# The decoder layer: the parts of x stored once and loaded by later stages, queries and keys transposed before they are split

## The chip, the cores and the metric

One Trainium2 chip, of which the kernel uses one core. The metric is the time of one execution on the device in microseconds (us); lower is better. Three runs of the kernel before took 1255.81, 1256.64 and 1258.46 us, median 1256.64.

Engine names are those of the profile: PE is TensorE's matmul, PEld its weight load, DVE VectorE, ACT ScalarE, POOL GpSimd, SP SyncE, from which all transfers (DMAs) of this kernel are issued.

## The reference

One decoder layer over 2048 tokens, model width 1024, head width 64. Both mixers have eight heads; mixer A has two heads of keys and values.

```python
hdn  = rmsnorm(x, norm_gain)
proj = einsum("bsd,de->bse", hdn, w_in)
q_a, k_a, v_a, g_a, q_b, k_b, v_b, g_b = split(proj)
q, k = rope(rmsnorm(q, ...)), rope(rmsnorm(k, ...))      # per head, both mixers
o_a = banded_attention(q_a, k_a, v_a, 127, sinks) * silu(g_a)
o_b = dilated_attention(q_b, k_b, v_b) * silu(g_b)       # (128,1), (512,4), (2048,16), merged
out = x + einsum("bse,ed->bsd", concat([o_a, o_b]), w_out)
```

Mixer A is causal attention with a window of 128 tokens and a learnt sink per head. Mixer B attends under three pairs of window and stride; the three results are merged by weights from their softmax denominators.

## The kernel before, in words

**Two parts for each operand.** A matmul takes each float32 operand as a high part, rounded to fp32r, and a low part, the rest. One product is three matmuls, high by high, high by low and low by high (`mm3`, L241 to L244). Everything that goes into a matmul is thus split first: the high part by a copy on ScalarE, the low part by a subtraction.

**Stages.** The work runs in eight stages: four of mixer B (a pair of heads each), two of mixer A (four query heads each) and two of the output projection (half of the output's columns each). A stage goes through four blocks `sb` of two halves; a half `hf` is 256 tokens, so a stage has eight halves. In a half, for each 128 tokens (`tt`), the projection takes eight chunks of x with three matmuls of 384 columns each (L244), and then the gates are made in the same way with 256 columns, once in B and twice in A.

**x.** x comes transposed from `in_xT`. `x_load` (L145 to L149) loads four chunks of a half into the tile `xs` (512 KB, two loads a half; in the output stages from the mixers' results `mx`), and `x_split` (L151 to L158) makes `xh` on ScalarE and `xl` on GpSimd or, for the second half of the chunks, in halves 0 to 5, on VectorE: four splits of 128x512 a half. Each stage loads and splits x anew for itself, one half ahead of its use. `xs` has two buffers, `xh` and `xl` six each. The very first half is split in `first_half`.

**Queries and keys.** `norm_rope` (L406) squares the projected values and applies the rotary tables (result `t1`, called t in the profile); `norm_factors` (L434) makes the factors `fac` of the per-head norm by a power on GpSimd (L182); `norm_split` (L441) multiplies `t1` by them on VectorE (L447) and splits the result into the tile `hl`, high parts on ScalarE (L456 queries, L457 keys, twice each), low parts on GpSimd (L458, L459). `qk_transposes` (L463) then transposes the parts on TensorE by the fp32r identity `idr`: in B four blocks for each 128 tokens (L475) and two for the low keys (L499); in A four (L485) and two (L490, L491) for each 128 tokens. ScalarE moves the transposed parts from PSUM (tile `po`) into `Q`, `qc`, `KK` and `klz` (L477, L478, L487, L493, L494, L502). In A, `klz` (`KL` in the code) has keys in one half of the partitions only. GpSimd also casts `Q` into `qc` in B (L479).

**Order.** The transposes of a half run in `finish`, which is deferred into the next half, behind its projection. Attention runs as a pipeline of units that `advance` slips between the projection's steps; the cost of a stage (`pcost`) sets how fast. A scheduler puts each engine's instructions into a fixed order when the kernel is built; all transfers stand in one queue of SP. Scores are L590 and L591 (windows) and L808 and L809 (strides), the probabilities' transposes L619, L625, L719, L828 (fp32, by `idf`), their parts L573 and L574 (`pth`, `ptl`).

**Others.** Weights come in `stg` tiles (three buffers) and are split into `wh`, `wl`. The three results of mixer B are merged on GpSimd with rows of weights that are written to DRAM (`rD`) and read back into all partitions (`Rb`): `o1c` by `Rb` (L899), `osum` by `Rb` (L904), their sum (L905), and the product with the gate (L906). At the start, GpSimd also clears the `klz` tiles (L90).

Of the kernel before, what the change touches and what calls it, by code (L numbers as in the profile page):

```python
# [21 lines left out]
XB = 6  # L22
# [6 lines left out]
def f32(ap):  # L29
    return ap.bitcast(F32)  # L30
# [3 lines left out]
def hybrid_layer(ctx, tc, xT, xn, x, wB, wA, wO, ng, gains, sinks, rot, masks, ident, out):  # L34
# [16 lines left out]
    idr = const.tile([128, 128], F32R, name="idr")  # L51
# [21 lines left out]
    def late_constants(part):  # L73
# [5 lines left out]
        nc.scalar.activation(idr, idf, AF.Copy)  # L79
# [12 lines left out]
    rs_row = [dram([256], f"rsr{hf}") for hf in range(8)]  # L92
    mx = [dram([128, KC, 256], f"mx{hf}") for hf in range(8)]
# [50 lines left out]

    def x_load(si, hf, g):  # L145
        src = mx[hf] if STAGES[si][0] == "O" else xT[hf]
        f = xp.tile([128, 4, 256], F32, name="xs")
        nc.sync.dma_start(f, src[:, 4 * g:4 * g + 4, :])
        XS[si, hf, g] = f  # L149

    def x_split(si, hf, g):  # L151
        f = XS[si, hf, g // 2][:, 2 * (g % 2):2 * (g % 2) + 2]
        h = xp.tile([128, 2, 256], F32R, name="xh", bufs=XB)
        l = xp.tile([128, 2, 256], F32R, name="xl", bufs=XB)
        nc.scalar.activation(h, f, AF.Copy)  # L155
        eng = nc.gpsimd if g < 2 or hf >= 6 else nc.vector
        eng.tensor_tensor(l, f, f32(h), op=OP.subtract)  # L157
        XG[si, hf, g] = (h, l)  # L158

    def first_half():  # L160
        for g in range(4):
            if g % 2 == 0:
                XS[0, 0, g // 2] = xp.tile([128, 4, 256], F32, name="xs")
            f = XS[0, 0, g // 2][:, 2 * (g % 2):2 * (g % 2) + 2]
            h = xp.tile([128, 2, 256], F32R, name="xh", bufs=XB)
            l = xp.tile([128, 2, 256], F32R, name="xl", bufs=XB)
# [4 lines left out]
            XG[0, 0, g] = (h, l)  # L171
# [74 lines left out]
    def proj(si, sb):  # L246
# [22 lines left out]
        for half in range(2):  # L269
            hf = 2 * sb + half  # L270
            nx = next_half(si, hf)
            xg = [XG.pop((si, hf, g)) for g in range(4)]
            TC, TS = TB.pop((si, hf))
            if nx:
                x_load(*nx, 0)
            t1s = []
            un = wk.tile([128, 2, nh], F32, name="un")
            for tt in range(2):
# [12 lines left out]
                if tt == 0 and nx:  # L291
                    x_load(*nx, 1)
# [44 lines left out]
            hls = norm_split(kind, nq, nk, t1s, fac)  # L337
            if si == 0 and hf < 7:
                rb_make(hf + 1)
            deferred.append(lambda half=half, hls=hls: finish(si, sb, half, hls))  # L340

    def finish(si, sb, half, hls):
# [3 lines left out]
        if half == 0 and sb > 0:  # L346
# [3 lines left out]
            for h in range(nk):  # L350
                hs = slice(64 * h, 64 * h + 64)
                nc.scalar.activation(KL[hs, h, :, 0, :], f32(pl[hs, h, :, 4, :]), AF.Copy)
        yield from qk_transposes(si, sb, half, hls)
# [87 lines left out]
    def norm_split(kind, nq, nk, t1s, fac):  # L441
        nh = nq + nk
        n = nh * 64
        hls = []
        for tt, t1 in enumerate(t1s):
            t1v = t1[:, :n].rearrange("p (h d) -> p h d", d=64)
            nc.vector.tensor_tensor(t1v, t1v, fac[:, tt, :, None].to_broadcast([128, nh, 64]), op=OP.mult)  # L447
            hl = wk.tile([128, 11, 64], F32R, name="hl", bufs=2)
            k0 = 2 * nq
            if kind == "A":  # L450
                hi, lo = hl[:, 0:8:2, :], hl[:, 1:8:2, :]
            else:
                hi, lo = hl[:, 0:4:3, :], hl[:, 1:3, :]
            khi = hl[:, k0:k0 + 2 * nk, :].rearrange("p (h a) d -> p h a d", a=2)
            klo = hl[:, k0 + 2 * nk:k0 + 3 * nk, :]
            nc.scalar.activation(hi, t1v[:, :nq], AF.Copy)  # L456
            nc.scalar.activation(khi, t1v[:, nq:, None, :].to_broadcast([128, nk, 2, 64]), AF.Copy)  # L457
            nc.gpsimd.tensor_tensor(lo, t1v[:, :nq], f32(hi), op=OP.subtract)  # L458
            nc.gpsimd.tensor_tensor(klo, t1v[:, nq:], f32(khi[:, :, 0, :]), op=OP.subtract)  # L459
            hls.append(hl)  # L460
        return hls

    def qk_transposes(si, sb, half, hls):  # L463
        kind, _ = STAGES[si]
        KK, KL = K[si, sb]
        q = Q[si, sb]
        i0 = 2 * half

        for tt, hl in enumerate(hls):
            i = i0 + tt  # L470
            if kind == "B":
                blocks = [hl[:, 2 * b:2 * b + 2, :] for b in range(4)]
# [567 lines left out]
```

## Time and profile before

| | |
|---|---|
| median of three runs | 1256.64 us |
| the profiled execution's own time | 1261.51 us |
| its span in the profile | 1259.4 us |
| mean granted TensorE clock | 0.969 |
| busy: PE, DVE, ACT, POOL | 1174.8, 850.7, 834.7, 680.4 us |
| loaded and stored by the SP queue | 219.37 MB |

How to read it: the span is one execution, taken by the hardware profiler; busy times are sums over an engine's instructions, of which many lie beside one another. The stages begin at about 0, 151, 314, 487, 661, 866, 1045 and 1156 us (first projection of the stage). A wait's row names the waiting engine, its instruction and what ended the wait, then the sum in us, the number and the longest. A group's row has the line, the engine, the operation, output and inputs with partitions x elements and type, the count, then the sum in us and the mean in ns of one, then the idle time ahead of them. Matmuls' ends are modelled, so that starts are the better reading. The granted clock is a share of full speed.

### The profile page before, as it was taken

What the parts mean: (1) busy time and instruction counts of PE and PEld (TensorE: products, weight loads), DVE (VectorE), ACT (ScalarE), POOL (GpSimd) and SP (SyncE); (2) the same over time, 40 slices, a digit from 0 to 9 for tenths busy, and PEclk for the clock granted to TensorE, in tenths of its full rate; (3) what the DMA queues carried; (4) which work ended last, traced back from release to release, by engine and by line L of the source; (5) the groups of instructions that cost most, each with busy time, mean ns of one, the idle gap of its engine ahead of it and who ended that gap; (6) DMA issues with size and microseconds to landing.
All of it is one profiled execution on the core that took longest, in us unless ns stands there. A gap on an engine that the chain in (4) does not pass through costs nothing.

```text
span 1259.4 us, 25438 instructions
## 1 busy us (share of the span) xinstructions
PE 1174.8 (93%) x8328; PEld 1141.3 (91%) x8328; DVE 850.7 (68%) x2288; ACT 834.7 (66%) x2418; POOL 680.4 (54%) x788
## 2 busy tenths in 40 slices
PE   6898979899899798899998999999999999999899
PEld 5898979899799798888997999898899998999898
DVE  5676768678677678776777788789868877522221
ACT  6477868678677687676777677677776776522221
POOL 4886734566645574536576567565655554333122
PEclk9899989999899899899998999999999999999999
DMA  7454677877687667687775764545333225566561
GB/s 215 120 166 127 193 226 212 229 200 212 182 250 207 210 190 201 189 244 204 199 210 172 228 203 143 150 137 167 114 97 94 80 89 165 163 192 211 166 191 69
DMA packets 196883, 220.98 MB, mean 175 GB/s; under 512 B 34312, under 2 KB 143632, under 8 KB 196752
## 3 DMA queue, kind: packets, MB, share of 16 engines
q1 hardware_dynamic: 196752, 219.37, 59.3%
q8 instruction: 66, 1.08, 0.4%
q14 instruction: 65, 0.53, 0.1%
HBM read 164.44 MB, written 54.86 MB: 174 GB/s over the span
## 4 chain that ended last, share of the span: by engine, by line
PE 55%; DMA 16%; DVE 10%; ACT 8%; POOL 6%; issue 3%; SPq 2%; POOLq 0%; ACTq 0%; DVEq 0%
PE pj L244 39%; DMA xs<-in_xT 3%; DMA Rb<-rD 2%; DMA stg<-in_wB 2%; PE po L849 2%; DMA stg<-in_wO 2%; DMA stg<-in_wA 2%; PE sc L590 1%; PE sc L591 1%; PE po L645 1%; PE pt L828 1%; PE po L735 1%; PE pt L719 1%; ACT P L599 1%; DVE ptl L574 1%
## 5 line engine op out<-in xcount | busy, mean ns | idle before, releaser
L244 PE MATMUL pj<-wh,xh 128*128 128x384 f32 (+1 forms) x1008 | 332.8, 332 | 12.2 <-ACT wh L104 5.5
L244 PE MATMUL pj<-wl,xh 128*128 128x384 f32 (+1 forms) x1008 | 334.4, 332 | 0.8 <-DVE wl L102 0.7
L244 PE MATMUL pj<-wh,xl 128*128 128x384 f32 (+1 forms) x1008 | 333.4, 331 | 1.3 <-DVE xl L157 1.3
L157 POOL TENSOR_TENSOR xl<-xs,xh 128x512 fp32r<-128x512 f32 x158 | 210.3, 1341 | 146.3 <-ACT xh L155 136.6
L155 ACT ACTIVATE xh<-xs 128x512 fp32r<-128x512 f32 x252 | 154.5, 629 | 123.6 <-PE pj L244 100.6
L244 PEld LDWEIGHTS pj<-wh,xh 128*128 128x128 f32 x1008 | 194.0, 193 | 15.7 <-ACT wh L104 5.8
L244 PEld LDWEIGHTS pj<-wl,xh 128*128 128x128 f32 x1008 | 194.8, 193 | 3.2 <-DVE wl L102 1.1
L244 PEld LDWEIGHTS pj<-wh,xl 128*128 128x128 f32 x1008 | 194.4, 193 | 3.0 <-DVE xl L157 1.6
L574 DVE TENSOR_TENSOR ptl<-pt,pth 128x512 fp32r<-128x512 f32 (+3 forms) x232 | 142.0, 619 | 35.5 <-ACT pth L573 31.8
L244 PE MATMUL pj<-xh,wgh 128*128 128x256 f32 x496 | 147.7, 298 | 17.9 <-DVE V L311 12.0
L244 PE MATMUL pj<-xh,wgl 128*128 128x256 f32 x496 | 145.8, 294 | 0.0
L244 PE MATMUL pj<-xl,wgh 128*128 128x256 f32 x496 | 145.4, 293 | 0.0
L573 ACT ACTIVATE pth<-pt 128x512 fp32r<-128x512 f32 (+3 forms) x232 | 123.1, 543 | 23.1 <-PE pt L719 8.1
L431 POOL TENSOR_TENSOR t<-t,t 128x256 f32<-128x256 f32 (+1 forms) x96 | 78.1, 814 | 77.9 <-DVE t L422 57.2
L244 PEld LDWEIGHTS pj<-xh,wgh 128*128 128x128 f32 x496 | 97.8, 197 | 19.7 <-ACT klz L502 5.9
L244 PEld LDWEIGHTS pj<-xl,wgh 128*128 128x128 f32 x496 | 97.8, 197 | 0.6
L244 PEld LDWEIGHTS pj<-xh,wgl 128*128 128x128 f32 x496 | 97.4, 196 | 0.9 <-DVE wgl L105 0.2
L814 ACT ACTIVATE P<-P,scD 128x256 f32<-128x256 f32 (+3 forms) x128 | 71.6, 560 | 33.6 <-DVE scD L813 32.9
L157 DVE TENSOR_TENSOR xl<-xs,xh 128x512 fp32r<-128x512 f32 x94 | 76.9, 823 | 21.1 <-ACT xh L155 20.5
L447 DVE TENSOR_TENSOR t<-t,fac 128x256 f32<-128x256 f32 (+1 forms) x96 | 67.4, 710 | 30.8 <-POOL fac L182 23.7
L182 POOL TENSOR_TENSOR fac<-un,mhalf 128x8 f32<-128x8 f32 (+1 forms) x48 | 85.4, 1779 | 2.5
L813 DVE CUSTOM_DVE_ANT_0 P<-sc,mk 128x256 f32<-128x256 f32 (+3 forms) x128 | 61.1, 484 | 32.2 <-PE sc L809 31.5
(188 smaller groups left out, 3082.8 us busy)
## 6 DMA issues: line engine op xcount, KB each, us to landing
xs<-in_xT SPq DMA_DIRECT2D x94, 512.0 KB
xs<-mx SPq DMA_DIRECT2D x32, 512.0 KB
vd<-V SPq DMA_DIRECT2D x64, 128.0 KB
qd<-qc SPq DMA_DIRECT2D x32, 256.0 KB
TT<-tab SPq DMA_DIRECT2D x32, 256.0 KB
cv<-vd SPq DMA_DIRECT2D x32, 256.0 KB
cq<-qd SPq DMA_DIRECT2D x32, 256.0 KB
ck<-kd SPq DMA_DIRECT2D x64, 128.0 KB
```

The lines of the kernel that those rows point to most:

```text
L155: nc.scalar.activation(h, f, AF.Copy)
L157: eng.tensor_tensor(l, f, f32(h), op=OP.subtract)
L182: nc.gpsimd.tensor_tensor(y, u, mhalf.to_broadcast([128, n]), op=OP.pow)
L244: nc.tensor.matmul(o, a, b, start=first and n == 0, stop=last and n == 2, skip_group_check=True)
L431: nc.gpsimd.tensor_tensor(t1[:, :n], t1[:, :n], t2[:, :n], op=OP.add)
L447: nc.vector.tensor_tensor(t1v, t1v, fac[:, tt, :, None].to_broadcast([128, nh, 64]), op=OP.mult)
L573: nc.scalar.activation(hi, pt, AF.Copy)
L574: nc.vector.tensor_tensor(lo, pt, f32(hi), op=OP.subtract)
L590: nc.tensor.matmul(sc[:, j, :], q[h // 2][:, h % 2, i, :], kw, start=True, stop=False)
L813: nc.vector.tensor_tensor_reduce(pd, o[:, :m], m2[:, 512 - m:], -0.125, BIG, OP.add, OP.min, nb)
L814: nc.scalar.activation(pd, pd, AF.Exp, bias=nb, scale=-1.0, accum_out=l)
L849: nc.tensor.matmul(po[:, o:o + w], a, b, start=n_ == 0, stop=n_ == len(seq) - 1, skip_group_check=True)
```

## The change

**x.** The high and the low part of two chunks now share one tile `x` of 128x1024, which is also the shape of a raw load, with nine buffers for both (`XB` from 6 to 9). In the first stage, when a half comes into use, `x_use` stores its four tiles of parts to DRAM (`xd`, 512 KB each). Stages 1 to 5 (`kept`) load these four tiles for each half instead of the two raw ones, all four at the start of the half before, and split nothing. The output stages split as before.

**Queries and keys.** `norm_scale` only multiplies by `fac`. `qk_transposes` transposes the unsplit `t1` in fp32 by `idf`: four blocks a half in B, four and two of 64 rows in A. ScalarE copies the result from PSUM to the SBUF tile `F` (tag `ob`, now two buffers, shared with the units' outputs) and makes the high parts from it, GpSimd the low parts, each for 64 partitions and 256 tokens. `idr` goes. In A the keys' low parts now stand in both halves of the partitions, and the scores read `KL[:, h % 2]`.

```diff
+    def x_parts():
+        t = xp.tile([128, 2, 2, 256], F32R, name="x", bufs=XB)
+        return t, t[:, 0], t[:, 1]
+    def kept(si):
+        return 0 < si and STAGES[si][0] != "O"
     def x_load(si, hf, g):
+        if kept(si):
+            for k in (2 * g, 2 * g + 1):
+                t, h, l = x_parts()
+                nc.sync.dma_start(f32(t).rearrange("p a c n -> p (a c n)"), xd[hf][:, k])
+                XG[si, hf, k] = (t, h, l)
+            return
...
     def x_split(si, hf, g):
+        if kept(si):
+            return
...
+    def x_use(si, hf):
+        ts = [XG.pop((si, hf, g)) for g in range(4)]
+        if si == 0:
+            for g in range(4):
+                nc.sync.dma_start(xd[hf][:, g], f32(ts[g][0]).rearrange("p a c n -> p (a c n)"))
+        return [t[1:] for t in ts]
...
-            xg = [XG.pop((si, hf, g)) for g in range(4)]
+            xg = x_use(si, hf)
             if nx:
                 x_load(*nx, 0)
+                if kept(nx[0]):
+                    x_load(*nx, 1)
...
-            nc.scalar.activation(hi, t1v[:, :nq], AF.Copy)
-            nc.scalar.activation(khi, t1v[:, nq:, None, :].to_broadcast([128, nk, 2, 64]), AF.Copy)
-            nc.gpsimd.tensor_tensor(lo, t1v[:, :nq], f32(hi), op=OP.subtract)
-            nc.gpsimd.tensor_tensor(klo, t1v[:, nq:], f32(khi[:, :, 0, :]), op=OP.subtract)
...
+        def queries(tile, h, src):
+            a, b = (hi64, lo64) if h else (lo64, hi64)
+            o = tile[:, h, i0:i0 + 2, :]
+            nc.scalar.activation(o[a], src[a], AF.Copy)
+            nc.gpsimd.tensor_tensor(o[b], src[a], f32(o[a]), op=OP.subtract)
+        def staged(pt):
+            f = wk.tile([128, 2, 2, 128], F32, name="ob", bufs=2)
+            nc.scalar.activation(f, pt, AF.Copy)
+            return f
+        if STAGES[si][0] == "B":
+            pt = ps.tile([128, 2, 2, 128], F32, name="po", bufs=2)
+            for b in range(2):
+                for tt, t1 in enumerate(t1s):
+                    nc.tensor.transpose(pt[:, b, tt, :], t1[:, 128 * b:128 * b + 128], idf)
+            F = staged(pt)
+            for h in range(2):
+                queries(q[0], h, F[:, 0])
+            pk = F[:, 1].rearrange("p i (r u) -> p i r u", u=32)
+            for h, (a, b) in enumerate(((lo64, hi64), (hi64, lo64))):
+                nc.scalar.activation(keys(KK, h)[a], pk[a], AF.Copy)
+                nc.scalar.activation(keys(KK, h)[b], pk[a], AF.Copy)
+                nc.gpsimd.tensor_tensor(keys(KL, h)[a], pk[a], f32(keys(KK, h)[a]), op=OP.subtract)
...
-                lw = KL[:, kh, :, k0:k0 + 2, :].rearrange("p r a u -> p a r u")
+                lw = KL[:, h % 2, :, k0:k0 + 2, :].rearrange("p r a u -> p a r u")
...
-    pcost = {"B": 4 * 8 * 490 + 2 * 8 * 330 + 4 * 340, "A": 4 * 8 * 490 + 4 * 8 * 330 + 4 * 340, "O": 4 * 8 * 650}
+    pcost = {"B": 4 * 8 * 490 + 2 * 8 * 330 + 2 * 436, "A": 4 * 8 * 490 + 4 * 8 * 330 + 2 * 654, "O": 4 * 8 * 650}
```

The SP queue near the start of the program, before: `xs` is the raw x of the second half, `TT` and `tab` the rotary tables, `stg` the weights, `idf`, `mk` and `sk` the identity, the masks and the sinks.

```order
L75 DMA gt<-in_gains 128x512
L393 DMA TT<-in_rot 128x4x64
L131 DMA stg<-in_wB 128x2x128 x3
L148 DMA xs<-in_xT 128x1024
L78 DMA idf<-in_ident 128x128
L80 DMA mk<-in_masks 128x768
L148 DMA xs<-in_xT 128x1024
L399 DMA tab_0_220<-TT 128x512
L131 DMA stg<-in_wB 128x2x128
L81 DMA sk<-in_sinks 128x8
```

The same place after; `xd` is the stored parts of the first half.

```order
L74 DMA gt<-in_gains 128x512
L415 DMA TT<-in_rot 128x4x64
L130 DMA stg<-in_wB 128x2x128 x3
L177 DMA xd_100<-x 128x1024 x4
L421 DMA tab_0_223<-TT 128x512
L130 DMA stg<-in_wB 128x2x128
L160 DMA x<-in_xT 128x1024 x2
L77 DMA idf<-in_ident 128x128
L78 DMA mk<-in_masks 128x768
L79 DMA sk<-in_sinks 128x8
```

The four stores and the table's store now stand ahead of both raw loads of the second half, and the identity behind them.

GpSimd's order at a D merge in the third stage, before: `hl` are the low parts, L431 is the rotary sum, L437 and L182 make the factors.

```order
L899 TENSOR_TENSOR o1c<-o1c,Rb 128x512
L431 TENSOR_TENSOR t_5742<-t_5742,t_5743 128x256
L479 CAST qc<-Q 128x8x32
L458 TENSOR_TENSOR hl<-t_5375,hl 128x128
L904 TENSOR_TENSOR osum<-osum,Rb 128x512
L459 TENSOR_TENSOR hl<-t_5375,hl 128x128
L458 TENSOR_TENSOR hl<-t_5470,hl 128x128
L459 TENSOR_TENSOR hl<-t_5470,hl 128x128
L905 TENSOR_TENSOR osum<-osum,o1c 128x512
L437 TENSOR_TENSOR un<-un,eps_84 128x8
L906 TENSOR_TENSOR osum<-osum,gc 128x512
L182 TENSOR_TENSOR fac<-un,mhalf 128x8
```

The same merge after: L920 and L925 to L927 are the merge's lines, L459, L453 and L201 the factors', L481 and L500 the low parts of queries and keys.

```order
L920 TENSOR_TENSOR o1c<-o1c,Rb 128x512
L459 TENSOR_TENSOR un<-un,eps_83 128x8
L453 TENSOR_TENSOR t_5438<-t_5438,t_5439 128x256
L201 TENSOR_TENSOR fac<-un,mhalf 128x8
L925 TENSOR_TENSOR osum<-osum,Rb 128x512
L926 TENSOR_TENSOR osum<-osum,o1c 128x512
L927 TENSOR_TENSOR osum<-osum,gc 128x512
L481 TENSOR_TENSOR Q<-ob,Q 64x256 x2
L500 TENSOR_TENSOR klz_89<-ob,KK 64x2x4x32 x2
```

The factors stand ahead of the three `osum` instructions now, and the low parts behind them.

More of the change, by code (lines that the diff above doesn't have):

```diff
@@ L78, in late_constants @@
         nc.sync.dma_start(idf, ident)
-        nc.scalar.activation(idr, idf, AF.Copy)
         nc.sync.dma_start(mk, masks)
@@ L467, in qk_transposes @@
         i0 = 2 * half
[L469 to L472, printed above, removed]
-                pt = ps.tile([128, 4, 128], F32R, name="po", bufs=2)
-                for b, a in enumerate(blocks):
-                    nc.tensor.transpose(pt[:, b, :], a, idr)
-                pv = f32(pt).rearrange("p h (r u) -> p h r u", u=32)
-                nc.scalar.activation(q[0][:, :, i, :], f32(pt)[:, 0:2], AF.Copy)
-                nc.scalar.activation(KK[:, :, :, i + 1, :], pv[:, 2:4], AF.Copy)
+        lo64, hi64 = slice(0, 64), slice(64, 128)
@@ L523, in proj_out @@
             nx = next_half(si, hf)
-            xg = [XG.pop((si, hf, g)) for g in range(4)]
+            xg = x_use(si, hf)
             if nx:
```

106 lines of the change are left out of this document (46 added, 60 removed).

## The prediction

> **What bounds the kernel now.** I read the page first, then the table of windows by stage, the timeline of PE, the groups by form and the waits.
>
> From the page: busy time of each engine, the row of DMA shares in 40 slices, the queue, the chain by engine.
>
> ```profile
> PE 1174.8 (93%) x8328; PEld 1141.3 (91%) x8328; DVE 850.7 (68%) x2288; ACT 834.7 (66%) x2418; POOL 680.4 (54%) x788
> DMA  7454677877687667687775764545333225566561
> q1 hardware_dynamic: 196752, 219.37, 59.3%
> PE 55%; DMA 16%; DVE 10%; ACT 8%; POOL 6%; issue 3%; SPq 2%; POOLq 0%; ACTq 0%; DVEq 0%
> ```
>
> TensorE is busy 93% of the 1259.4 us span, no other engine over 68%: it is the bound, but not the whole of it. Only 55% of the chain that ended last is PE; 16% is transfers (0.16 × 1259.4 = 202 us), nearly all on one queue, which moves 219.37 MB. The chain passes through transfers wherever PE's next input is late.
>
> The windows, one stage a row: the four B stages, the two A stages (the two output stages, which the change hardly touches, are left out).
>
> ```profile
> core 0: us, PE busy (x) PEld busy (x) DVE busy (x) ACT busy (x) POOL busy (x), PEclk, DMA share, GB/s
> 0.00:151.00 151.00, 130.66 (x855) 127.01 (x856) 103.11 (x244) 104.28 (x282) 106.75 (x147) 0.95 0.56 161
> 151.00:314.00 163.00, 153.32 (x1055) 149.58 (x1054) 120.07 (x338) 124.21 (x364) 87.38 (x110) 0.97 0.77 217
> 314.00:487.00 173.00, 158.46 (x1065) 153.62 (x1064) 123.52 (x339) 127.20 (x369) 98.86 (x118) 0.94 0.72 207
> 487.00:661.00 174.00, 159.32 (x1079) 153.66 (x1078) 125.88 (x342) 128.63 (x377) 96.83 (x120) 0.95 0.74 209
> 661.00:866.00 205.00, 194.30 (x1373) 187.67 (x1371) 162.17 (x470) 150.65 (x459) 126.43 (x142) 0.98 0.58 172
> 866.00:1045.00 179.00, 173.97 (x1257) 168.07 (x1257) 143.52 (x417) 132.04 (x421) 102.77 (x105) 1.00 0.32 101
> ```
>
> PE's idle time in stages 1 to 5 is 9.7 + 14.5 + 14.7 + 10.7 + 5.0 = 54.6 us, and 20.3 us in stage 0. The last two columns matter as much: in stages 1 to 3 the transfers take 0.72 to 0.77 of all that the 16 DMA engines have. Dividing GB/s by share gives what a full share would move: 217/0.77 = 282, 207/0.72 = 288, 209/0.74 = 282; I take 285 GB/s.
>
> **The change part by part.** First, the transposes. PE's timeline (start, busy time) with a group of four fp32 transposes (idf) and one of four and one of two fp32r transposes (idr), each among matmuls of known spacing:
>
> ```profile
> 233.97 0.60 PE L619 MATMUL pt<-idf,P 128*128 128x128 f32 x4
> 234.32 0.36 PE L808 MATMUL sc<-ck,cq 128*128 128x256 f32 x1
> 234.52 0.28 PE L809 MATMUL sc<-cl,cq 128*128 128x256 f32 x1
> 234.64 0.34 PE L808 MATMUL sc<-ck,cq 128*128 128x384 f32 x1
> ...
> 235.69 0.46 PE L475 MATMUL po<-idr,hl 128*128 128x128 f32 x4
> 235.98 0.41 PE L244 MATMUL pj<-wl,xh 128*128 128x384 f32 x1
> 236.23 0.34 PE L244 MATMUL pj<-wh,xl 128*128 128x384 f32 x1
> 236.41 0.34 PE L244 MATMUL pj<-wh,xh 128*128 128x384 f32 x1
> ...
> 239.21 0.29 PE L499 MATMUL po<-idr,hl 128*128 128x128 f32 x2
> 239.33 0.41 PE L244 MATMUL pj<-wl,xh 128*128 128x384 f32 x1
> 239.58 0.49 PE L625 MATMUL pt<-idf,P 128*128 128x128 f32 x3
> ```
>
> Starts are the safe reading, since ends are modelled. Four fp32r transposes and the matmul behind them take 236.23 − 235.69 = 0.54 us; one such matmul's slot is 236.41 − 236.23 = 0.18, which leaves 0.36. Two take 239.58 − 239.21 − 0.18 = 0.19. Four fp32 ones take 234.52 − 233.97 − 0.12 (the 256-column slot, 234.64 − 234.52) = 0.43: unsplit transposes cost a little more each, but there are fewer. A B half goes from 0.36 + 0.36 + 0.19 = 0.91 to 0.43, an A half from 2 × (0.36 + 0.19) = 1.10 to 0.43 + 0.22 = 0.65. With 32 B halves and 16 A halves that is 15.4 + 7.2 = 22.6 us of PE work gone. At least the PE share of the chain comes off the time (0.55 × 22.6 = 12), at most all; I take **−18**, since PE is 93% busy.
>
> Second, the splits of x. The groups of ScalarE's copies, GpSimd's and VectorE's subtractions (count; busy, mean ns; idle before):
>
> ```profile
> L155 ACT ACTIVATE xh<-xs 128x512 fp32r<-128x512 f32 x252 | 154.5, 629 | 123.6 <-PE pj L244 100.6 <-DMA xs<-in_xT 12.8 <-issue 4.3
> L157 POOL TENSOR_TENSOR xl<-xs,xh 128x512 fp32r<-128x512 f32 x158 | 210.3, 1341 | 146.3 <-ACT xh L155 136.6 <-DMA xs<-mx 7.3
> L157 DVE TENSOR_TENSOR xl<-xs,xh 128x512 fp32r<-128x512 f32 x94 | 76.9, 823 | 21.1 <-ACT xh L155 20.5
> ```
>
> A stage has 8 halves of 4 splits: 32 × 0.629 = 20.1 us of ScalarE, 20 × 1.341 = 26.8 of GpSimd, 12 × 0.823 = 9.9 of VectorE; over stages 1 to 5 that is 101, 134 and 49 us. None of these engines is the bound, so this is worth only what PE waits for them or behind them: nothing at least; at most half of the 54.6 us of PE idle time, since the other half stands behind weights, D merges and small transfers that stay. The groups say that the splits mostly wait themselves (ScalarE 100.6 us for PE to free a buffer), so they are early rather than late. I take a fifth, **−11**. Next late are the loads, counted below.
>
> Third, the staging.
>
> ```profile
> L458 POOL TENSOR_TENSOR hl<-t,hl 128x128 fp32r<-128x128 f32 x64 | 32.9, 515 | 16.9 <-ACT hl L456 16.8
> L458 POOL TENSOR_TENSOR hl<-t,hl 128x256 fp32r<-128x256 f32 x32 | 26.8, 837 | 19.9 <-ACT hl L456 18.1 <-PE pt L719 1.8
> L459 POOL TENSOR_TENSOR hl<-t,hl 128x64 fp32r<-128x64 f32 x32 | 12.8, 401 | 0.0
> L477 ACT ACTIVATE Q<-po 128x256 fp32r<-128x256 f32 x64 | 24.2, 377 | 8.0 <-PE po L475 8.0
> L502 ACT ACTIVATE klz<-po 64x256 fp32r<-64x256 f32 x64 | 23.9, 374 | 0.6
> L573 ACT ACTIVATE pth<-pt 128x512 fp32r<-128x512 f32 x144 | 84.7, 593 | 13.0 <-PE pt L719 7.2 <-PE pt L828 2.4 <-PE pt L619 1.7
> ```
>
> L477 and L502 show that half the partitions save nothing: the length along the partition sets the time. So a B half's ScalarE work is now 0.593 + 6 × 0.374 = 2.84 us in 7 instructions where ten of about the latter size stood: ScalarE is relieved, which at 76% or less of any stage is worth nothing. A 64x256 subtraction on GpSimd is not in the trace; its bounds are 0.401 (128x64) and 0.837 (128x256), and I take 0.837 by the same reading. A B half's GpSimd work goes from 4 × 0.515 = 2.06 (the keys' two are of the queries' size) to 4 × 0.837 = 3.35, an A half's from 2 × (0.837 + 0.401) = 2.48 to 6 × 0.837 = 5.02: +1.29 × 32 + 2.54 × 16 = +82 us against the 134 that leave, a net relief. But it moves. Before, low parts were made ahead of the transposes, and one evacuation lay between transpose and score. Now the path is 0.59 (staging) + 0.37 (high part) + 0.84 (low part), and 2.8 to 4.5 us for the last low part of a B half. By the order of PE about 41 matmuls, over 8 us, lie between these transposes and the first score that needs the parts, in a few places 3 to 5. I take **+4**, bounds 0 and +12 (32 B and 16 A halves at a quarter of a microsecond).
>
> Fourth, GpSimd's order around the D merge, as the rows of the order show it: the factors (fac) stood behind the osum multiplies, now ahead. In the chain, and in the waits:
>
> ```profile
> 424.69 1.29 POOL osum L904
> ...
> 428.46 1.29 POOL osum L906
> 429.75 1.61 POOL fac L182
> ```
>
> ```profile
> POOL o1c L899 <- DMA Rb<-rD: 58.3, 15, 8.2
> DVE t L447 <- POOL fac L182: 23.7, 9, 5.7
> ```
>
> VectorE waits 23.7 us for factors, at worst 5.7 at a time, and here the chain runs through it; the osum multiplies of 1.29 us and a second wait for Rb no longer stand ahead. Of 23.7 I take a quarter, **−6** (0 to −12).
>
> Fifth, the transfers. Stage 0 stores 8 × 4 × 512 KB = 16.8 MB; each stage 1 to 5 loads 16.8 MB in place of 8.4. That is 58.7 MB on a queue that moves 219. Needs at 285 GB/s: stage 0 161 × 151 = 24.3 + 16.8 = 41.1 MB, 144 us of 151; stage 1 217 × 163 = 35.4 + 8.4 = 43.8 MB, 154 of 163; stages 2 and 3 155 of 173 and 157 of 174; stage 4 153 of 205; stage 5 93 of 179. The large loads have a whole half (some 20 us) to land and are not late themselves; the small transfers (Rb, vd, the weights, the reloaded q and k), which issue in order behind four 512 KB blocks, are. The chain holds 202 us of transfers: a tenth longer is 20, none is the floor, a fifth is 40. I take **+18**. At the start of the program the second half's raw loads stand behind four stores and a table, but a wait of PE for rst goes, since the clears of klz now stand behind it: ±0.
>
> Sum: −18 − 11 + 4 − 6 + 18 = −13 us. The profiled execution took 1261.51 us, 4.9 (0.4%) above the median 1256.64; the terms are differences, so I put them on the median: 1243.6, say 1244. With the terms' bounds, two or three of them off at a time, this case alone reaches from 1230 to 1258.
>
> **The rivals.** *The relief pays in full*: all 22.6 of PE, half the idle time (27), the 6 of the factors, less 4 and 18: −34, 1223. For it: PE at 93%. Against: the splits wait more than they are waited for.
>
> *The queue becomes the bound.* The highest digit in the row of DMA shares is 8, so no stretch of 31 us ran at 0.9 or above. If 0.88 is as far as it goes, stages 0 to 3 need 144/0.88 = 164, 175, 176 and 178 us: 13 + 12 + 3 + 4 = +32, less some 10 that the A stages still gain from transposes and factors: 1279, slower. It decides from a needed share of about 0.9, which stages 0 and 1 pass (0.95, 0.94). Against it: stores and loads of 4 KB rows may be cheaper than the mean packet of these rows. The Trainium skill's HBM Reference, Specifications (TRN2), has a core that streams alone at about 425 GB/s; by that stage 0 would need 97 us and this rival would fall, but the rows here give 282 to 288 and decide.
>
> *GpSimd takes ScalarE's place between transposes and scores*: its stream halts behind every wait for Rb (58.3 us in 15 waits), and low parts queued there are late. If a third of those waits, 18 us, reaches PE, the sum is +5: about 1261. Against it: the 41 matmuls of cover. The Trainium skill's GPSIMD Engine Reference, Performance versus the Vector engine, puts elementwise work on VectorE as about twice as fast; the groups here give 1341 to 823, 1.63, and by that rule this rival is the likelier for low parts than for splits, which had a buffer's lead.
>
> **How the numbers follow.** Forecast 0.43, full relief 0.15, queue 0.28, GpSimd 0.14. About 0.2% (2.5 us) is what a measurement of this kernel can tell from no change. Faster: 0.40 of the forecast's 0.43, 0.15, and 0.03 of the third rival's, 0.58; same: 0.02 and 0.06, 0.08; slower: 0.28, 0.05 and 0.01, 0.34. The range reaches from below full relief (1216) to above the queue's case (1284).
>
> **What would show it.** PE's busy time down by about 20 us at a like clock; no split of x in stages 1 to 5; the fp32 transposes 32 × 4 + 16 × 6 in number; DMA shares near 0.9 in stages 0 to 3. If stages 0 and 1 are longer than 151 and 163 us while 4 and 5 are shorter, the queue rival holds. If PE's waits name the low parts by GpSimd for over 10 us, the third does. If PE's idle time in stages 1 to 5 falls below 30 us, relief in full. I am wrong altogether if PE's busy time does not fall.

## The result, and the profile after

The changed kernel takes 1277.77 us in the median of four runs (1276.47 to 1279.90), against 1256.22 for the kernel before: a ratio of 1.0170, 95% interval 1.0149 to 1.0191, or 21 us slower. 1244 was forecast, as faster. The time lies where the second rival put it (1279, the queue as the bound). The profiled execution has a span of 1274.3 us, 14.9 more than the one before the change; the lengths of stages below are of these two.

From the page of the changed kernel, the rows that answer to those of before: busy times, shares of the transfers in 40 slices, the queue, the chain by engine.

```profile
PE 1163.2 (91%) x8040; PEld 1125.7 (88%) x8040; DVE 795.7 (62%) x2228; ACT 762.4 (60%) x2103; POOL 621.9 (49%) x720
DMA  8978998987998978898878975566453525366552
q1 hardware_dynamic: 212880, 278.10, 71.6%
PE 43%; DMA 27%; DVE 10%; ACT 8%; POOL 5%; issue 4%; SPq 3%; POOLq 0%; ACTq 0%; DVEq 0%
```

All four compute engines are less busy than before, and the time is longer. What grew is the queue, from 219.37 to 278.10 MB, and with it the transfers' share of the chain that ended last, from 16% to 27%. The first twenty digits, which were 4 to 8, are now 7 to 9.

The windows by stage; the two last rows are the output stages.

```profile
core 0: us, PE busy (x) PEld busy (x) DVE busy (x) ACT busy (x) POOL busy (x), PEclk, DMA share, GB/s
0.00:148.00 148.00, 129.50 (x807) 124.76 (x807) 104.15 (x241) 101.57 (x255) 110.74 (x140) 0.94 0.87 280
148.00:321.50 173.50, 155.44 (x1025) 150.06 (x1024) 109.95 (x329) 111.14 (x315) 71.60 (x92) 0.95 0.87 259
321.50:494.00 172.50, 155.84 (x1024) 149.05 (x1025) 113.35 (x329) 111.12 (x317) 77.58 (x97) 0.97 0.88 257
494.00:673.50 179.50, 155.99 (x1021) 150.22 (x1020) 110.75 (x328) 111.42 (x317) 79.43 (x101) 0.94 0.85 247
673.50:879.00 205.50, 190.37 (x1327) 183.75 (x1326) 154.23 (x462) 137.85 (x398) 118.89 (x138) 0.98 0.71 215
879.00:1054.00 175.00, 169.89 (x1196) 165.44 (x1197) 128.07 (x400) 121.51 (x356) 94.85 (x101) 0.98 0.44 143
1054.00:1172.70 118.70, 111.09 (x884) 108.77 (x883) 50.85 (x106) 47.60 (x113) 46.95 (x40) 0.97 0.54 168
1172.70:1274.30 101.60, 95.12 (x769) 93.60 (x768) 24.32 (x39) 20.17 (x38) 21.90 (x17) 0.98 0.47 152
```

The first output stage before:

```profile
1045.00:1156.00 111.00, 108.60 (x888) 107.61 (x887) 48.77 (x107) 47.14 (x116) 38.07 (x31) 0.98 0.59 182
```

Against 151, 163, 173, 174, 205, 179, 111 and 103.4 before: stage 1 lost 10.5 us, stage 3 5.5 and the first output stage 7.7; stage 5 gained 4 and stage 0 gained 3, though it now stores 16.8 MB more. In stages 0 to 3 the transfers take 0.85 to 0.88 of the 16 engines, where three of them had 0.72 to 0.77.

What busy transfer engines do to the order of things stands in the chain of stage 2 (start, us, what):

```profile
359.24 5.86 DMA x<-xd
365.11 7.86 DMA ck<-kd
373.06 0.36 PE sc L829
...
374.45 0.52 SPq L803
375.01 0.45 SPq L806
375.82 0.46 SPq L809
376.33 7.26 DMA cl<-ld
383.71 7.72 DMA x<-xd
391.45 2.70 DMA cl<-ld
```

For 35 us the end of the program is set almost by transfers alone: a block of stored parts, the keys `ck` of the strided scores, the low parts `cl`, a block again. A `ck` that took 3.67 us in the chain of stage 1 before takes 7.86 here, right behind a block of 512 KB. Over the whole chain, 50 transfers of 4.04 us in the mean became 71 of 4.87.

### The profile page after: what moved, and what is told of

The parts are those of the page before. It is cut to its first block, busy times and chain, and to the rows that moved or that the text cites. A ratio compares the mean times of both kernels' runs of the same rounds, so it can differ in the third digit from the quotient of the medians.

```text
span 1274.3 us, 24514 instructions
## 1 busy us (share of the span) xinstructions
PE 1163.2 (91%) x8040; PEld 1125.7 (88%) x8040; DVE 795.7 (62%) x2228; ACT 762.4 (60%) x2103; POOL 621.9 (49%) x720
## 3 DMA queue, kind: packets, MB, share of 16 engines
q1 hardware_dynamic: 212880, 278.10, 71.6%
## 4 chain that ended last, share of the span: by engine, by line
PE 43%; DMA 27%; DVE 10%; ACT 8%; POOL 5%; issue 4%; SPq 3%; POOLq 0%; ACTq 0%; DVEq 0%
PE pj L263 30%; DMA Rb<-rD 5%; DMA stg<-in_wB 3%; DMA x<-in_xT 3%; DMA stg<-in_wA 2%; DMA x<-xd 2%; PE po L756 2%; PE pt L740 2%; DVE t L466 2%; DMA rD<-rr 2%; DMA stg<-in_wO 1%; PE sc L612 1%; DVE ptl L595 1%; PE sc L611 1%; PE po L870 1%
## 5 line engine op out<-in xcount | busy, mean ns | idle before, releaser
L263 PE MATMUL pj<-wh,x 128*128 128x384 f32 (+1 forms) x2016 | 556.6, 331 | 11.7 <-ACT wh L103 6.9
L263 PEld LDWEIGHTS pj<-wh,x 128*128 128x128 f32 x2016 | 376.8, 193 | 16.9 <-ACT wh L103 7.1
L263 PE MATMUL pj<-wl,x 128*128 128x384 f32 (+1 forms) x1008 | 333.5, 331 | 0.0
L263 PE MATMUL pj<-x,wgh 128*128 128x256 f32 x992 | 205.8, 296 | 5.6 <-DVE V L333 5.3
L263 PEld LDWEIGHTS pj<-wl,x 128*128 128x128 f32 x1008 | 194.6, 193 | 2.7 <-DVE wl L104 0.4
L263 PEld LDWEIGHTS pj<-x,wgh 128*128 128x128 f32 x992 | 164.9, 198 | 7.6 <-ACT Q L480 3.6
L263 PE MATMUL pj<-x,wgl 128*128 128x256 f32 x496 | 146.0, 294 | 1.0 <-DVE wgl L104 1.0
L594 ACT ACTIVATE pth<-pt 128x512 fp32r<-128x512 f32 (+3 forms) x232 | 121.5, 539 | 28.0 <-PE pt L740 12.8
L263 PE MATMUL pj<-wgh,x 128*128 128x256 f32 x496 | 130.8, 286 | 0.3 <-ACT wgh L100 0.3
L453 POOL TENSOR_TENSOR t<-t,t 128x256 f32<-128x256 f32 (+1 forms) x96 | 78.4, 817 | 97.9 <-DVE t L444 58.7
L481 POOL TENSOR_TENSOR Q<-ob,Q 64x256 fp32r<-64x256 f32 x96 | 75.6, 788 | 61.0 <-ACT Q L480 54.8
L263 PEld LDWEIGHTS pj<-x,wgl 128*128 128x128 f32 x496 | 98.1, 198 | 1.8 <-DVE wgl L104 1.4
L263 PEld LDWEIGHTS pj<-wgh,x 128*128 128x128 f32 x496 | 95.7, 194 | 0.5 <-ACT wgh L100 0.5
L201 POOL TENSOR_TENSOR fac<-un,mhalf 128x8 f32<-128x8 f32 (+1 forms) x48 | 85.0, 1771 | 3.0
```

The lines of the kernel that those rows point to most:

```text
L201: nc.gpsimd.tensor_tensor(y, u, mhalf.to_broadcast([128, n]), op=OP.pow)
L263: nc.tensor.matmul(o, a, b, start=first and n == 0, stop=last and n == 2, skip_group_check=True)
L453: nc.gpsimd.tensor_tensor(t1[:, :n], t1[:, :n], t2[:, :n], op=OP.add)
L481: nc.gpsimd.tensor_tensor(o[b], src[a], f32(o[a]), op=OP.subtract)
L594: nc.scalar.activation(hi, pt, AF.Copy)
```

## The experiments

Every time stands beside runs of the kernel before on the same chip; its median was 1255 to 1258 throughout, so that the ratios are compared. In us, a ratio is multiplied by 1256.

Three theories stood at first: **1**, the added traffic makes other transfers late; **2**, GpSimd's low parts now stand between the transposes and the scores; **3**, the buffers that raw loads and parts share make loads late.

### The halves of the change, and half of the loads

**e1_keep**, the stored parts alone, and **e2_trans**, the transposes alone: each has its own hunks of the diff and none of the other's; e1 has `XB = 8`.

> The stored and loaded parts of x alone, on the kernel before (eight shared buffers instead of nine, for room; queries and keys split before the transposes as before). Theory 1, the transfers: the 58.7 MB more on the queue make the small transfers late; this kernel carries all of them without the transposes' relief, so it is slower than the change itself: 1280 to 1295 us. Theory 2, GpSimd: the low parts between the transposes and the scores cost the time; without them this kernel is at 1245 to 1257. Theory 3, the shared buffers: the output stages are 6 to 10 us longer, the rest is as before: 1262 to 1268.

> The unsplit transposes with staging and low parts on GpSimd alone, x split anew in every stage as before. Theory 1: the 16 us of PE work that leave come off nearly in full, 1238 to 1246. Theory 2: GpSimd has the splits of x as well as 82 us more of low parts, so it is slower than before, 1262 to 1285. Theory 3: as theory 1.

Measured: e1_keep 1291.19 us, ratio 1.0294 (1.0261 to 1.0326); e2_trans 1268.19, ratio 1.0097 (1.0071 to 1.0123). Both halves lose by themselves: the stored parts 37 us, the transposes 12. The first is theory 1's number; the second is theory 2's, and theory 1's gain of 10 to 18 us did not come.

**e3_half** takes the added traffic out of stages 1 to 5 and leaves every engine its instructions; half of x is left out of the projections there:

```diff
-            for k in (2 * g, 2 * g + 1):
-                t, h, l = x_parts()
-                nc.sync.dma_start(..., xd[hf][:, k])
-                XG[si, hf, k] = (t, h, l)
+            t, h, l = x_parts()
+            nc.sync.dma_start(..., xd[hf][:, 2 * g])
+            for k in (2 * g, 2 * g + 1):
+                XG[si, hf, k] = (t, h, l)
```

> The change, but a half of the stages 1 to 5 loads only two of its four tiles of parts, and each of them stands for two pairs of chunks, so half of x is left out of the projections there; the queue carries as much in these stages as before the change, and nothing is split. Theory 1: stages 1, 2 and 3 fall from 173.5, 172.5 and 179.5 to about 158 to 165 each, the time to 1235 to 1248. Theory 2: 1270 to 1278, the scores wait as before. Theory 3: 1268 to 1276, the output stages stay long.

Measured: 1242.33 us, ratio 0.9888 (0.9857 to 0.9918). From the change to this kernel it is 1.0170 − 0.9888 = 0.028, or 35 us, for 42 MB of loads. Its page and its windows (stages 1 to 4):

```profile
PE 1155.6 (93%) x8040; PEld 1122.4 (90%) x8040; DVE 796.1 (64%) x2228; ACT 761.3 (61%) x2103; POOL 620.1 (50%) x720
```

```profile
150.80:317.80 167.00, 154.97 (x1025) 150.32 (x1022) 108.85 (x329) 110.51 (x315) 72.28 (x92) 0.96 0.76 221
317.80:487.20 169.40, 154.09 (x1023) 149.85 (x1023) 112.33 (x329) 111.60 (x317) 77.81 (x97) 0.96 0.76 213
487.20:655.00 167.80, 154.29 (x1022) 149.02 (x1023) 111.99 (x329) 111.64 (x317) 79.47 (x101) 0.97 0.76 214
655.00:850.70 195.70, 188.82 (x1323) 181.83 (x1324) 154.81 (x461) 136.85 (x396) 114.67 (x136) 0.99 0.61 182
```

ScalarE, VectorE and GpSimd do what they do in the changed kernel to within 2 us, the shares are back at 0.76, and stage 3 is 167.8 us long instead of 179.5, stage 4 195.7 instead of 205.5. The added loads are what separates these two kernels. Stages 1 to 3 are each 2 to 4 us longer than the 158 to 165 that I expected, so that the loads are not all that stood in their way.

**e9_keep_half** is the same edit on e1_keep:

> The stored parts alone, as in e1_keep (1291.19), but with half of the loads: each of two tiles stands for two pairs of chunks, so half of x is left out of the projections in stages 1 to 5. The queue carries there what it carried before the change, nothing is split, queries and keys are as before. Theory 1 as it stands after e3_half, that splits of x are little in the way of PE by themselves: 1248 to 1257. If taking the splits off the engines is worth what the forecast said without the transposes too: 1232 to 1246.

Measured: 1244.61 us, ratio 0.9896 (0.9850 to 0.9942). Taking the splits off the engines is thus worth 13 us when its traffic is paid for, without the transposes too, which is what the forecast's second term said (−11); it lies in the second of the two ranges above. The traffic on e1_keep costs 1.0294 − 0.9896, or 50 us. The windows of stages 1 to 4, of e1_keep:

```profile
152.60:330.90 178.30, 159.04 (x1057) 153.44 (x1056) 104.23 (x329) 110.73 (x339) 60.72 (x90) 0.93 0.83 246
330.90:509.70 178.80, 158.69 (x1076) 152.57 (x1074) 105.97 (x329) 112.13 (x339) 64.67 (x95) 0.97 0.83 248
509.70:686.70 177.00, 161.53 (x1075) 156.37 (x1076) 108.69 (x328) 111.67 (x340) 68.42 (x99) 0.94 0.84 250
686.70:895.40 208.70, 195.61 (x1360) 188.80 (x1360) 149.50 (x463) 135.53 (x424) 96.49 (x124) 0.96 0.70 212
```

and of e9_keep_half:

```profile
153.20:319.50 166.30, 155.69 (x1067) 151.73 (x1066) 104.67 (x329) 112.44 (x341) 58.62 (x88) 0.97 0.77 221
319.50:490.00 170.50, 157.63 (x1066) 152.48 (x1066) 108.50 (x329) 111.99 (x341) 67.73 (x97) 0.95 0.77 211
490.00:655.70 165.70, 154.89 (x1070) 150.61 (x1068) 106.62 (x329) 110.72 (x339) 69.34 (x102) 0.97 0.75 217
655.70:850.00 194.30, 189.82 (x1371) 185.09 (x1369) 149.74 (x459) 133.15 (x421) 96.80 (x122) 0.99 0.63 182
```

The four stages differ by 742.8 − 696.8 = 46 us, and PE's busy time in them by 674.9 − 658.0 = 17: waiting explains 29 us, and 17 are matmuls that take longer, 16 of them in the three stages (1, 3 and 4) where the granted clock is 0.93, 0.94 and 0.96 against 0.97, 0.97 and 0.99. Whether the transfers or the longer waits lower the clock was not separated.

### Traffic by itself

**e4_more** was to add the traffic to the kernel before, as a copy from DRAM to DRAM behind each load of x:

```diff
         nc.sync.dma_start(f, src[:, 4 * g:4 * g + 4, :])
+        if 0 < si < 6:
+            nc.sync.dma_start(dram([128, 4, 256], f"xe{si}_{hf}_{g}"), src[:, 4 * g:4 * g + 4, :])
```

> The kernel before, with a copy of the same 512 KB from DRAM to DRAM issued behind each load of x in stages 1 to 5, read by nobody: it carries 8.4 MB more a stage, as the change does, and computes as before. Theory 1: 15 to 35 us slower, 1272 to 1291, most of it in stages 1 to 3. Theories 2 and 3: within 5 us of before.

Measured: 1367.47 us, ratio 1.0889 (1.0844 to 1.0933), and not the experiment that was meant. Its windows up to stage 2:

```profile
0.00:251.30 251.30, 149.41 (x857) 141.25 (x858) 103.19 (x243) 106.63 (x283) 103.57 (x146) 0.78 0.84 263
251.30:418.20 166.90, 151.36 (x1044) 147.08 (x1043) 120.94 (x330) 123.46 (x360) 90.87 (x112) 0.98 0.75 213
418.20:596.10 177.90, 159.64 (x1071) 153.44 (x1071) 124.35 (x340) 126.85 (x372) 96.02 (x117) 0.96 0.72 202
```

A copy that waits for nothing is put at the program's front: all 80 are issued from 19.8 to 167.0 us, so that the 42 MB stand in stage 0, which takes 251 us instead of 151, and the two stages behind it are 4 and 5 us longer than before. **e8_more_in_stage** therefore stores the tile loaded before, so that each store waits for its place:

```diff
+        if 0 < si < 6:
+            pv = (si, hf, 0) if g else (si, hf - 1, 1) if hf else (si - 1, 7, 1)
+            nc.sync.dma_start(dram([128, 4, 256], f"xe{si}_{hf}_{g}"), XS[pv])
```

> The kernel before, with a store of the raw x tile that was loaded before into DRAM, read by nobody, behind each load of x in stages 1 to 5: 8.4 MB more a stage, inside the stages this time, since each store has to wait for its tile. Theory 1, the transfers: stages 1 to 3 grow by 5 to 13 us each, 1275 to 1300. If the traffic alone is harmless, and the change's cost comes from loads that are late or from buffers: within 6 us of before.

Measured: 1297.90 us, ratio 1.0345 (1.0291 to 1.0399), 43 us for 42 MB that nobody reads, beside the same computation. But these 43 us are not the traffic's alone. Most stores wait, at the head of the one queue, until the tile that they store has landed, and whatever stands behind them waits too. Among the queue's own waits:

```profile
SPq L151 <- DMA xs<-in_xT: 107.1, 48, 5.4
```

The longest sum of one such row before was 48.9 us. Nor did stages 1 to 3 grow by 5 to 13 us each: they are 182.8, 177.5 and 174.5 us long against 163, 173 and 174, the last with a share of 0.84. The price of the traffic rests on e3 and e9, 35 and 50 us.

**e10_act_queue** issues the loads of the changed kernel from ScalarE's queue (`nc.scalar.dma_start` for `xd`):

> The change with the loads of stored parts issued from ScalarE's queue, all else from SP's. If the small transfers are late because they stand in one queue behind four blocks of 512 KB: 1250 to 1266. If they are late because the 16 engines are shared whatever the queue: 1270 to 1285, with shares of 0.85 to 0.88 again.

Measured: 1287.51 us, ratio 1.0248 (1.0195 to 1.0301). The page has the loads on their own queue,

```profile
q1 hardware_dynamic: 189840, 194.20, 50.0%
q10 hardware_dynamic: 23040, 83.90, 20.5%
```

and the time is no better; it is above both ranges. This does not settle whether the place behind the blocks in one queue matters. Summed over its waits, PE in the changed kernel waits 58.2 us for VectorE and 27.8 for ScalarE, here 35.1 and 58.3 (e3_half: 37.6 and 28.7): the waits for VectorE are gone to e3_half's size, and the loads now stand in ScalarE's stream, for which PE waits instead. That both changes come from the new place of the loads is argued, not shown.

**e7_kept_a** loads stored parts in the A stages only (`kept` returns `STAGES[si][0] == "A"`), **e12_a_only** makes the transposes unsplit there only as well (with eight buffers, and the staging tile under the tag `hl` in place of `ob`, which has one buffer):

> The change, but only the two A stages load the stored parts; stages 1 to 3 load raw x and split it, as before. Theory 1, the transfers: the queue has room in the A stages (0.58 and 0.32 before), so these lose nothing by the loads, and stages 1 to 3 are those of e2_trans (168.5, 174.8, 172.3): 1250 to 1262, faster than the change and than e2_trans. Against it, if the loads cost time at any share: 1266 to 1278.

> The change for the two A stages alone: unsplit transposes and loads of stored parts there (eight shared buffers), the B stages as before but for the stores in stage 0. If the B stages are where the change loses, and the A stages with their idle queue gain what e7_kept_a showed (202.9 + 168.2 against 205 + 179): 1240 to 1250, faster than both kernels. If the stores of stage 0 or the first output stage (118.0 against 110.9) take it back: 1253 to 1262.

Measured: 1265.74 us, ratio 1.0058 (1.0028 to 1.0087), and 1266.54, ratio 1.0091 (1.0057 to 1.0125). Stage 5 is 168.2 and 173.2 us long against 179, as hoped, but neither kernel is faster, and e12 is above both of its ranges. In e7_kept_a stages 1 to 3, which were to be e2_trans's 168.5, 174.8 and 172.3, take 174.4, 177.4 and 174.1, and the first output stage 118.0 against 111. This row stands among ScalarE's waits there:

```profile
ACT x L168 <- DMA x<-in_xT: 78.0, 28, 6.3
```

Before, ScalarE waited 12.8 us, five times, for raw x. Where stages still load raw x through the buffers that raw tiles and parts now share, the raw loads land late. That this row is what takes the gain back is argued, not shown.

**e18_after_8** is the change with `XB = 8`:

> The change with eight shared buffers for x instead of nine, which e1_keep, e9_keep_half and e12_a_only had for room. If buffers cost, loads start later: 1283 to 1295, so that a part of e1_keep's 36 us is the missing buffer. If not: 1272 to 1282, as the change.

Measured: 1280.10 us, ratio 1.0171 (1.0129 to 1.0212), as the change: e1 and e9, with eight buffers, can be set beside it, and the ninth buffer is worth nothing here. Theory 3 is out for the kept stages.

### The transposes

**e5_trans_dve** and **e6_after_dve** put the low parts of queries and keys on VectorE (`nc.vector` for the three subtractions in `qk_transposes`), in e2_trans and in the change:

> The transposes alone, as in e2_trans (1268.19), but with the low parts of queries and keys subtracted on VectorE. If GpSimd costs the time there (its splits of x and its waits for Rb stand ahead of the low parts, and the scores wait 16.8 us for them): 1238 to 1252, the waits of PE for low parts under 5 us. If it is the longer path itself, from PSUM through the staging tile to high and then low parts, on whatever engine: 1258 to 1270.

> The change with the low parts of queries and keys on VectorE. GpSimd has no splits in stages 1 to 5 here, and scores wait 12.5 us for low parts. If GpSimd is a part of the cost: 1258 to 1268. If the transfers alone are: 1272 to 1280, with shares of the transfers as after the change, 0.85 to 0.88 in stages 0 to 3.

Measured: 1273.10 us, ratio 1.0123 (1.0078 to 1.0167), and 1274.81, ratio 1.0140 (1.0091 to 1.0188). Theory 2 falls: with GpSimd out of the path, e2_trans gains nothing (it is above both ranges) and the change four us. In e5 PE waits elsewhere, for V (17.7 us), the low parts of x (11.7) and the gates (7.1), all on VectorE, which is 90% and 93% busy in the A stages.

**e11_trans_psum** leaves the staging tile out: `queries` and the keys read `pt` in PSUM, ScalarE for the high, VectorE for the low parts. **e14_psum_spare** puts the staging copy back behind them, unread. **e13_psum_gp** is e11 with all low parts of x on GpSimd (`eng = nc.gpsimd`). **e15_after_psum** is e11's edit on the change.

> The transposes alone, as in e5_trans_dve (1273.1), but without the staging tile: ScalarE makes the high parts and VectorE the low parts straight from PSUM. If the longer path from the transposes to the scores is what the transposes' half of the change costs: 1248 to 1262. If it is the load on VectorE and the other engines, which carry the splits of x as well: 1265 to 1278.

> The transposes alone, parts made straight from PSUM (e11_trans_psum, 1258.47), and the low parts of x all on GpSimd, which is busy 47% there against VectorE's 75%; no traffic is added. If VectorE's load is what still hides the 16 us of PE work that the transposes save: 1240 to 1252, faster than both kernels. If not: 1255 to 1266.

> e11_trans_psum with the staging copy put back on ScalarE behind the high and low parts, into a tile that nobody reads: the same load on ScalarE as in e5_trans_dve (1273.1) and the path to the scores as short as in e11 (1258.47). If the path is what the staging costs: 1255 to 1263. If it is ScalarE's load or the longer hold of PSUM: 1268 to 1278.

> The whole change, but with both parts of queries and keys made straight from PSUM by ScalarE and VectorE, without the staging tile. If the staging costs here what it costs in the transposes alone (e5 less e11, 14.6 us): 1258 to 1268. If the transfers hide it, since the time goes by the queue in stages 1 to 3: 1270 to 1280.

Measured: e11 1258.47 us, ratio 1.0007 (0.9980 to 1.0033); e13 1269.94, 1.0105 (1.0068 to 1.0142); e14 1286.75, 1.0225 (1.0182 to 1.0268); e15 1277.75, 1.0167 (1.0126 to 1.0209). Without staging the transposes cost nothing, but return nothing either. The longer path need not be to blame: e14's path is e11's, and it is 27 us slower, more than expected of either answer. But its copy also holds PSUM and the tile `ob` longer, so that e14 does not show that the path costs nothing. Moving x's low parts off VectorE did not help: e13 is above both of its ranges. And e15 has the change's time: what the staging costs elsewhere is hidden where the transfers set the time.

### What an order alone moves

Every edit gives all engines a new order. **e16_before_pace** changes one number of the pacing of the kernel before (`own` for B from 4 * 2900 to 4 * 3500), **e17_after_pace** gives the change the `pcost` of before; the instructions stay the same.

> The kernel before with one number of the pacing of the B stages changed (own from 2900 to 3500): the same instructions in another order, a control for what an order alone can move. If differences of some 10 us between the variants here can come from the order alone: 6 us or more from before, either way. If the order is harmless, so that differences of that size are the edits': 1252 to 1262.

> The change with the pacing's costs (pcost) of before, the same instructions in an order of its own: the same control for the kernel after. If the order alone moves 6 us or more: outside 1271 to 1283. If it is harmless: within that.

Measured: 1260.71 us, ratio 1.0024 (1.0001 to 1.0046), and 1270.17, ratio 1.0098 (1.0066 to 1.0130). An order alone moved the kernel before by 3 us and the changed one by 9. Differences under some 9 us between two kernels here say little about their edit. The traffic's 35 and 50 us, and e14 against e11, stand well outside that, e9's 13 and e2's 12 narrowly. That the transposes gain nothing in the kernel before rests on all of their variants there (e2, e5, e11, e13, e14), of which none is faster. All of these split x in every stage; beside the stored parts it is otherwise, as the next section shows.

## Why the prediction was wrong, step by step

**The transposes (−18).** The count of PE's work was right. In the changed kernel's timeline,

```profile
244.33 0.60 PE L492 MATMUL po<-idf,t 128*128 128x128 f32 x4
244.69 0.49 PE L263 MATMUL pj<-x,wgh 128*128 128x256 f32 x2
245.01 0.29 PE L263 MATMUL pj<-x,wgl 128*128 128x256 f32 x1
```

four fp32 transposes take, reckoned as in the forecast, 245.01 − 244.33 − 2 × 0.12 = 0.44 us, against 0.43. PE's busy time is 19 us lower in e3_half (1155.6 against 1174.8), where the traffic of stages 1 to 5 is as before. The step that failed is that "PE is 93% busy", so that most of this comes off the time. The runs have the transposes in three settings; PE's idle time is the span less its busy time, without and with them, in us:

| x | ratio, parts transposed | ratio, unsplit transposed | PE idle | PE busy |
|---|---|---|---|---|
| split in every stage | 1 (before) | 1.0097 (e2) | 84.6, 98.9 | 1174.8, 1168.2 |
| stored, half of the loads | 0.9896 (e9) | 0.9888 (e3) | 70.5, 85.2 | 1173.4, 1155.6 |
| stored, all loads | 1.0294 (e1) | 1.0170 (the change) | 99.0, 111.1 | 1188.6, 1163.2 |

In each row PE waits 12 to 15 us more with the unsplit transposes. The forecast took the saved work off the time and had only the +4 of the staging for such waits; that is the step. In time the transposes cost 12 us in the first row and nothing in the second. Only beside all the loads did they gain, 16 us (e18_after_8, with e1's eight buffers, has 1.0171). The saving of busy time, 7, 18 and 25 us, went with the granted clock, 0.969 to 0.968, 0.968 to 0.972 and 0.957 to 0.965. Why it is largest beside all the loads is open.

**The splits of x (−11).** The size was right: −13 by e9_keep_half, with the stores of stage 0 in it. That is PE's idle time, 70.5 us against 84.6; the fifth that I took of it was a guess.

**The staging (+4).** The rival that GpSimd takes ScalarE's place had the right rows and no force. In the changed kernel PE waits for its low parts:

```profile
PE sc L612 <- POOL klz L500: 6.3, 4, 3.2
PE sc L611 <- POOL Q L481: 6.2, 4, 2.1
```

12.5 us, over the 10 that I named as its sign; e6_after_dve takes these waits away and gains 4 us, no more than an order's worth. The rule of the Trainium skill's GPSIMD Engine Reference, Performance versus the Vector engine, by which VectorE is the better place, is not borne out in time here: e5_trans_dve follows it and is no faster, though one subtraction of 64x256 takes less there, 590 ns in the mean on VectorE against 788 on GpSimd in the changed kernel. The price of a low part was right, 788 ns against 837 taken:

```profile
L481 POOL TENSOR_TENSOR Q<-ob,Q 64x256 fp32r<-64x256 f32 x96 | 75.6, 788 | 61.0 <-ACT Q L480 54.8
```

What the staging copy itself costs is not settled: e11 against e5 says 15 us, e14 against e11 27, and neither the path's length nor ScalarE's load was separated from the longer hold of PSUM and from the order.

**The factors (−6).** Not so. VectorE's wait for them grew from 23.7 us:

```profile
DVE t L466 <- POOL fac L201: 70.7, 16, 10.2
```

They stand ahead of the `osum` multiplies now, but still behind `o1c`, which waits for Rb. That this is what holds them was not tried by itself. The added loads are not needed for it: the wait is 59.6 us in e9_keep_half and 59.5 in e3_half, but 26.2 in e2_trans, so that it came with the stored parts.

**The transfers (+18, 0 to +40).** This term was mis-sized: 35 us by e3_half against the change, 50 by e9 against e1. It alone turns the sign: with 35 in place of 18 the sum is +4. The rest of the way to +21 is the transposes, staging and factors, which were to bring −20: −13 of relief and +35 of traffic are +22, with nothing for these three. By the other way, −13, +50 and the transposes' −16, it is +21; the two prices of the traffic differ by what the transposes gain beside it. My working took a tenth of the chain's 202 us of transfers; but the rows that I had, 0.94 to 0.95 of the engines needed in stages 0 and 1, spoke for the rival, and the chain's transfers went to 27% of 1274 us, 344. The rival's own form was half right. Shares did stop at 0.85 to 0.88, as it said, and stage 1, for which it gave 175 us, took 173.5. Stage 0, for which it gave 164, took 148: the stored and loaded blocks of 4 KB rows move faster than the mean that I took. By the two queue rows, 58.7 MB more cost 0.716 × 1274.3 − 0.593 × 1259.4 = 166 us of all engines, 355 GB/s against my 285. That its 1279 was met is therefore luck: the +13 of stage 0 did not come, and 7.7 us stand in an output stage that it did not count. Nor did the time go by a lack of bandwidth alone: stages 1 and 3 lost 10.5 and 5.5 us at shares of 0.87 and 0.85, with a seventh of the engines' time left, while stages 0 and 2, at 0.87 and 0.88, lost nothing. The transfers on the chain became more and longer, as said above. PE itself waits only 6.5 us for transfers by name (4.5 in e3_half) and 58.2 for VectorE (37.6): how late transfers reach PE through VectorE's inputs was not followed. The 425 GB/s of the Trainium skill's HBM Reference, Specifications (TRN2), are reached by nothing here, where the highest of the 40 slices after the change has 315; by them I would have dropped the rival that won.

**The first output stage**, 7.7 us longer, was in no term. It is long in the change, e7 and e12 (118.7, 118.0, 116.9 us), not in e1, e2, e6 and e9 (110.2, 109.2, 108.8, 109.1), and in between in e15 (113.7) and in e3, e10, e17 and e18 (112.7 to 115.4). The shared buffers are in all three lists, and e6 has the change's loads as well; why it is long is open.

No version was found that beats the kernel before with the whole computation done; the two that are faster leave half of x out.

## What to carry to other kernels

Trading computation on idle engines for traffic is a good trade only where the transfers have room: here 8.4 MB more in each of stages 1 to 4 cost 46 us in all (e1 against e9), at shares that rose in stages 1 to 3 from about 0.76 to 0.83, while bandwidth was still left. Before such a change, take the relief without the traffic (half of the loads) as a kernel of its own, as e3 and e9 did. The traffic alone is harder to have: stores that nobody reads went to the program's front (e4) or brought a wait of their own into the queue (e8). Set the parts of a change beside each other with and without the other part, since their prices need not add up: the transposes cost 12 us, nothing, or gained 16. And measure how much a new order moves the time, before a few us are put down to an edit.

## What was not expected of the hardware

- With the added transfers PE lost time twice: by waiting, and by longer matmuls. 17 of the 46 us between e1 and e9 in stages 1 to 4 are PE's busy time, at granted clocks of 0.93 to 0.97 against 0.95 to 0.99. In e4's stage 0, where PE stood still for 102 of 251 us, the granted clock was 0.78.
- VectorE's subtraction of 64x256 is not slow, but held up. With both operands in SBUF it takes 590 ns in the mean (e5_trans_dve), with one in PSUM 421 (e11_trans_psum); the shortest, the median and the longest in ns say more, first of e5, then of e11:

```profile
L457 DVE TENSOR_TENSOR Q<-ob,Q x96: 418/421/1561, 51.2 to 1071.1; 64x256 fp32r<-64x256 f32 x96
```

```profile
L457 DVE TENSOR_TENSOR Q<-po,Q x96: 407/420/428, 50.3 to 1055.5; 64x256 fp32r<-64x256 f32 x96
```

Of e5's 128 such subtractions (queries of both mixers), the 79 with no GpSimd instruction beside them took 420 ns in the mean, the 49 with one 830. In e11 the 63 beside GpSimd took 421.
